# Transposing the two heads of an attention pair together, with each product in its own bank

## The chip, the cores and the metric

The kernel runs on one core of a Trainium2 chip. The metric is the device time of one execution in microseconds, compared as the median of the runs. Five engines appear below: PE (matrix products and transposes; PEld is its weight load), DVE (vector work), ACT (activations and copies), POOL (general work), and SP, which issues most transfers from HBM.

## The reference

One layer of a hybrid decoder on 256 tokens of width 1024, in fp32. Three mixers read one combined projection, a gated merge joins them, and two layer norms frame a large MLP.

```python
proj = x @ w_in[i]
aq, ak, av, iq, ik, iw, bq, bk, bv, cq, ck, cv = jnp.split(proj, SPLIT_POINTS, axis=-1)
o_a = dsa_mixer(...)        # 6 heads, 64 keys chosen by an indexer, one shared k and v
o_b = dilated_mixer(...)    # 4 slots, three dilated query groups over shared keys
o_c = moba_mixer(...)       # 6 heads, at 256 tokens plain causal attention
merged = (gates[:, :, 0] * (o_a @ w_br_a[i]) + gates[:, :, 1] * (o_b @ w_br_b[i])
          + gates[:, :, 2] * (o_c @ w_br_c[i]))
x = layer_norm(ALPHA * x + merged @ w_out[i], ln1_g[i], ln1_b[i])
h = jnp.square(jax.nn.relu(x @ w_up[i])) @ w_down[i]
ple = jax.nn.sigmoid(x @ w_ple_gate[i]) * (p[i] @ w_ple[i])
x = layer_norm(ALPHA * x + h + ple, ln2_g[i], ln2_b[i])
```

What the change touches is the end of each head's attention: the softmax's weights are transposed and multiplied with the values, 16 times (4 slots, 6 heads of `o_c`, 6 heads of `o_a`), two heads to a pair.

## The kernel before

Every fp32 matrix is split into a rounded high part and the rest (high on ACT, L75; low on DVE and POOL, L79), and a product is three matmuls in a reduced fp32 form. Weights arrive in units of 128 x 1024 through five `raw` buffers; a load waits until the split of the unit five places ahead of it has freed a buffer. `W.get` keeps the splits four units ahead of the product.

The program has stages. The first computes queries, keys and values from x, the indexer and its top 64 (a generator that DVE works off between other things), then the pairs: two of slots (`slots`, L351), three of `o_c` (L470), three of `o_a` (L487). Between the pairs stand gate products and branch products (`fill`, L234), so that PE has work while a pair's softmax runs on DVE and ACT. Then come the merge of the branches (`merge`, L561), the product with `w_out`, the first layer norm (`ln1`, L630) with its own transposes (L644), the gate of the per-layer embedding (`pg`), the MLP up (L693, L695) and down, and the second layer norm.

One head goes through these steps. `logits` (L264) fills two PSUM banks, one for each head of the pair. DVE adds the bias and takes the extreme; ACT takes the exponential; DVE the reciprocal; ACT scales the rows (L335). `attend` (L308) then transposes the three 128 x 128 blocks of the weights `P` into a bank (L314), ACT copies them to `pt` as the high part (L315), DVE makes the low part (L316), two matmuls form the product with the values (L318, L319), ACT copies the lower half of it out (L322), and DVE adds the halves (L323, L324) into the pair's `o`. When both heads are in `o`, `pair_out` (L326) splits `o` into `op`, which the branch products and the merge read.

PSUM has eight banks: three for `mm`, five named b0 to b4. Logits turn through b0, b1, b2; all transposes use b3; all products with the values use b4. So the second head's transposes wait until the first head's are out of b3.

The order on each engine is made by a scheduler that plays the program against its own idea of durations; `tc.keep_in_program_order` pins an instruction behind the one recorded before it on its engine, `tc.issue_after` behind a named one, and `high_priority` moves one ahead. All else is free to move, so that a change in one stage can move rows in the next.

Of the kernel before, what the change touches and what calls it, by code (L numbers as in the profile page):

```python
# [11 lines left out]
F32 = mybir.dt.float32  # L12
F32R = mybir.dt.float32r
ALU = mybir.AluOpType
# [6 lines left out]
S = 256  # L21
# [20 lines left out]
FIRST = 4  # L42
# [53 lines left out]
def hybrid_layer(ctx: ExitStack, tc: tile.TileContext, x0, xn, pT, wqk, wva, wvb, wg, wbc, wba,  # L96
                 wout, wup, wdq, wdn, wpg, wple, lnrow, rel, mask, out):
    nc = tc.nc
    pe, act, dve, pool = nc.tensor, nc.scalar, nc.vector, nc.gpsimd
# [10 lines left out]
    def turns(ids):  # L110

        while True:
            for i in ids:
                yield banks.tile([128, 512], F32, name=f"b{i}", tag=f"b{i}")

    ps_s, ps_t, ps_v, ps_a = turns((0, 1, 2)), turns((3,)), turns((4,)), turns((0, 1, 3, 2, 4))

    ident = keep.tile([128, 128], F32, name="ident")
    make_identity(nc, ident)
# [9 lines left out]
    t = banks.tile([128, 512], F32, name="b4", tag="b4")  # L129
# [43 lines left out]
    for t in TASKS:  # L173
# [4 lines left out]
        elif t in "gcao":  # L178
            u, w, n = {"g": (u_g, wg, 1024), "c": (u_bc, wbc, 640), "a": (u_ba, wba, 768),
                       "o": (u_out, wout, 1024)}[t]  # L180
# [14 lines left out]
    pts = [p1.tile([128, 2, 384], F32R, name=f"pt{i}") for i in range(2)]  # L195
# [84 lines left out]
    V = p1.tile([128, 2, 11, 128], F32R, name="V")  # L280
    iw = p1.tile([128, 2, 8], F32, name="iw")
    op = pm.tile([128, 8, 2, S], F32R, name="op")
# [22 lines left out]

    n_pt = [0]

    def attend(P, vh, o, h):  # L308

        pt = pts[n_pt[0] % 2]  # L310
        n_pt[0] += 1
        t = next(ps_t)
        for c in range(3):
            pe.transpose(t[:, 128 * c:128 * c + 128], P[:, 128 * c:128 * c + 128], ident)  # L314
        act.copy(pt[:, 0], t[:, 0:384])  # L315
        dve.tensor_tensor(pt[:, 1], t[:, 0:384], pt[:, 0].bitcast(F32), op=ALU.subtract)  # L316
        v = next(ps_v).rearrange("p (a s) -> p a s", a=2)
        pe.matmul(v, lhsT=V[:, 0, vh], rhs=pt[:, :, 0:256], start=True, stop=False)  # L318
        pe.matmul(v[:, :, 128:256], lhsT=V[:, 1, vh], rhs=pt[:, :, 256:384], start=False,  # L319
                  stop=True)  # L320
        x = wk2.tile([64, 2, S], F32, name="ov", tag="ov")
        act.copy(x, v[64:128])  # L322
        dve.tensor_tensor(x, v[0:64], x, op=ALU.add)  # L323
        dve.tensor_tensor(o[64 * h:64 * h + 64], x[:, 0], x[:, 1], op=ALU.add)  # L324

    def pair_out(o, kt):  # L326
        hi = act.copy(op[:, kt, 0], o)
# [3 lines left out]
    def scale_rows(P, den):  # L331
        r = sm.tile([128, 2], F32, name="r", tag="r")
        dve.reciprocal(r, den)
        for b in range(2):
            act.mul(P[:, QC[b]], P[:, QC[b]], r[:, b:b + 1])  # L335


    def head(s, t0, t1, vh, o, h):
        e = wk.tile([128, 384], F32, name="e", tag="e")
        mx = sm.tile([128, 2], F32, name="mx", tag="mx")  # L340
        den = sm.tile([128, 2], F32, name="den", tag="den")
        for b, t in enumerate((t0, t1)):
            dve.tensor_tensor_reduce(e[:, QC[b]], s[h][:, QC[b]], t, op0=ALU.add, op1=ALU.min,
                                     scale=1.0, scalar=-GONE, accum_out=mx[:, b:b + 1])
        for b in range(2):
            act.activation(e[:, QC[b]], e[:, QC[b]], AF.Exp, bias=mx[:, b:b + 1], scale=-1.0,
                           accum_out=den[:, b:b + 1])
        scale_rows(e, den)
        attend(e, vh, o, h)

    def slots(qs, k, Ts, vh, o):  # L351

        es = [wk2.tile([128, 3, 384], F32, name="eb", tag="eb") for _ in range(2)]
        mxs = [sm.tile([128, 2, 3], F32, name="mxb", tag="mxb") for _ in range(2)]
        for g in range(3):
            s = logits(qs[g], k)
            for h in range(2):
                for b, t in enumerate((Ts[h][:, g, 128:256], Ts[h][:, g, :])):
                    dve.tensor_tensor_reduce(es[h][:, g, QC[b]], s[h][:, QC[b]], t, op0=ALU.add,
                                             op1=ALU.min, scale=1.0, scalar=-GONE,  # L360
                                             accum_out=mxs[h][:, b, g:g + 1])
        for h in range(2):
            e = es[h]
            m = sm.tile([128, 2], F32, name="mx", tag="mx")
            den = sm.tile([128, 2], F32, name="den", tag="den")
            dve.tensor_reduce(m, mxs[h], axis=AX.X, op=ALU.min)
            for b in range(2):
                act.activation(e[:, :, QC[b]], e[:, :, QC[b]], AF.Exp, bias=m[:, b:b + 1],
                               scale=-1.0, accum_out=den[:, b:b + 1])
            pool.tensor_tensor(e[:, 0], e[:, 0], e[:, 1], op=ALU.add)  # L370
            added[0] = pool.tensor_tensor(e[:, 0], e[:, 0], e[:, 2], op=ALU.add).ins
            scale_rows(e[:, 0], den)
            attend(e[:, 0], vh + h, o, h)

# [9 lines left out]
    with ExitStack() as begin:  # L386
        st = begin.enter_context(tc.tile_pool(name="st", bufs=1, side="right"))
        sh, sl = (st.tile([128, KT, FIRST * 128], F32R, name=n) for n in ("sh", "sl"))
        g0 = G.rearrange("p i s -> p (i s)").rearrange("p (k c) -> p k c", k=KT)
        cut = [((0, 384), (384, 768)) if k == 0 else ((0, 768),) for k in range(KT)]  # L390
        with tc.high_priority(offset=1000):
            for k in range(KT):
                for i, (a, b) in enumerate(cut[k]):
                    e = nc.scalar if i else nc.sync
                    e.dma_start(g0[:, k, a:b], x0[k, :, a:b])
            for k in range(KT):
                act.copy(xh[:, k], g0[:, k, 0:S])
                for a, b in cut[k]:
                    a = max(a, S)
                    act.copy(sh[:, k, a - S:b - S], g0[:, k, a:b])  # L400
                dve.tensor_tensor(xl[:, k], g0[:, k, 0:S], xh[:, k].bitcast(F32), op=ALU.subtract)
                dve.tensor_tensor(sl[:, k], g0[:, k, S:], sh[:, k].bitcast(F32), op=ALU.subtract)
        first = [next(ps_s if f < 3 else ps_t)[:, 0:S] for f in range(FIRST)]
        for k in range(KT):
            for i, (w, x) in enumerate(((sh, xh), (sh, xl), (sl, xh))):
                for f in range(FIRST):
                    pe.matmul(first[f], lhsT=w[:, k, 128 * f:128 * f + 128], rhs=x[:, k],  # L407
                              start=k == i == 0, stop=k == KT - 1 and i == 2)
        iq = [q_pair(ps, 0.125) for ps in first]
    tp, wk, wk2, sm = (right(n, b) for n, b in (("tp", 3), ("wk", 3), ("wk2", 2), ("sm", 6)))  # L410
# [13 lines left out]
    for j in range(4):  # L424
        s = logits(iq[j], kI)
        r = wk2.tile([128, 768], F32, name="ri", tag="eb")
        r = r.rearrange("p (h k) -> p h k", h=2)
        for h in range(2):
            act.activation(r[:, h], s[h], AF.Relu)
            for b in range(2):  # L430
                n = 2 * j + h
# [15 lines left out]
    def opair():  # L447
        return wk2.tile([128, S], F32, name="o", tag="o")

    for j in range(2):  # L450
# [8 lines left out]
        o = opair()  # L459
# [10 lines left out]
    for j in range(3):  # L470
        ps = feat(13 + 2 * j)
        k = k_pair(ps)
        q = q_pair(feat(14 + 2 * j))
        s = logits(q, k)
        o = opair()
        for h in range(2):
            n = 2 * j + h
            if n % 3 == 0:
                T = toeplitz(18 + n, 1)
            head(s, T[:, n % 3, 128:256], T[:, n % 3], 5 + n, o, h)  # L480
            fill("g")
        pair_out(o, 5 + j)

# [2 lines left out]
    T = None  # L486
    for j in range(3):  # L487
        q = q_pair(feat(19 + j))
        s = logits(q, kA)
        o = opair()  # L490
        for h in range(2):
            n = 2 * j + h
            if n % 3 == 0:
                T = toeplitz(n, 1)
            ta = wk.tile([128, 384], F32, name="ta", tag="ta")
            with tc.issue_after(W.pool):
                pool.tensor_tensor(ta[:, 0:128], T[:, n % 3, 128:256], am[:, 0:128], op=ALU.add)
                pool.tensor_tensor(ta[:, 128:384], T[:, n % 3], am[:, 128:384], op=ALU.add)
            head(s, ta[:, 0:128], ta[:, 128:384], 0, o, h)
            fill("gg" if n == 0 else "gc")  # L500
        done = pair_out(o, j)
    fill("ggcc")
# [152 lines left out]
    for b in range(2):  # L655
        t = slice(b * 128, (b + 1) * 128)
# [31 lines left out]
    for f in range(32):  # L688
# [5 lines left out]
        for k in range(KT):  # L694
            pe.matmul(ps[:, :, 0], lhsT=lo[:, cs[k]], rhs=x1[:, :, k, 0], start=False,  # L695
                      stop=k == KT - 1)
# [3 lines left out]
        u, m = divmod(f, 4)  # L700
        if u >= QUADS:
            q = w2.tile([128, S], F32, name="q2", tag="q2")
            act.activation(q, r.rearrange("p b t -> p (b t)"), AF.Square)
            h = hT[:, f - 4 * QUADS]
# [21 lines left out]
        else:  # L726
            ts = [[qpool.tile([128, 2, S], F32R, name="q", tag="q")
                   .rearrange("p m (j t) -> p m j t", j=2) for _ in range(2)] for _ in range(2)]
# [61 lines left out]
    for x in order:  # L790
# [4 lines left out]
        else:  # L795
            i = x - NP + 2
# [20 lines left out]
    for i in range(early):  # L817
        x = order[i]
# [39 lines left out]
    for b, c, lo, hi in runs:  # L858
        cs = slice(*CUT[b][c])
        for i in range(lo, hi):  # L860
            h, l = ws[i]
# [102 lines left out]
```

## Time and profile before

| | |
|---|---|
| three runs | 434.8, 435.6, 436.42 us; median 435.6 |
| the profiled execution | 437.98 us |
| its span, first to last instruction | 436.2 us |
| granted TensorE clock over the span | 0.994 |
| busy PE, DVE, ACT, POOL | 425.1, 350.5, 276.2, 105.4 us |
| matmuls and transposes on PE | 2799 |

A row of a timeline has the start in us, the time, the engine, the line, the operation, what it writes and reads, and in square brackets the idle time ahead of it with what ended that. A matmul's own duration is longer than its step, since matmuls overlap; the step from start to start is what it costs PE.

### The profile page before, as it was taken

The page shows a single profiled execution, that of the slowest core. Times are in us where ns is not written, and L with a number is a line of the kernel's source. Part 1 is how long each engine was busy: PE and PEld are TensorE (multiplying, and loading weights), DVE is VectorE, ACT ScalarE, POOL GpSimd, SP SyncE. Part 2 cuts the span into 40 slices and gives each one's busy share as a digit, 9 for nine tenths or more (in the row PEclk, how much of TensorE's full clock was granted, in tenths as well). Part 3 has the DMA queues.
Part 4 walks back from the last instruction along what each step waited for, and adds up shares of the span by engine and source line. Part 5 has one row for each costly group of instructions (what it writes and reads, how often), then busy time and mean ns, then how long its engine had stood idle before and what let it go on. Part 6 is the DMA issues. An engine that isn't in the chain of part 4 may idle for free.

```text
span 436.2 us, 7669 instructions
## 1 busy us (share of the span) xinstructions
PE 425.1 (97%) x2799; PEld 386.0 (88%) x2799; DVE 350.5 (80%) x625; ACT 276.2 (63%) x490; POOL 105.4 (24%) x98
## 2 busy tenths in 40 slices
PE   8999999999999999999998999999999999999993
PEld 8999999999999999999886888888888888888882
DVE  5978987577476577879957779999988897998984
ACT  6775375586787777756524567788887855665500
POOL 2563355395434566400000000000100000000001
PEclk9999999999999999999999999999999999999997
DMA  8797756457654436455960875656795377758411
GB/s 298 291 326 234 230 173 191 150 189 250 183 151 145 128 109 187 144 192 178 400 246 0 288 237 185 187 180 203 277 268 187 115 207 269 200 192 278 155 41 57
DMA packets 27690, 86.39 MB, mean 198 GB/s; under 512 B 2884, under 2 KB 6892, under 8 KB 27268
## 3 DMA queue, kind: packets, MB, share of 16 engines
q1 hardware_dynamic: 25872, 79.54, 55.1%
q0 software_dynamic: 640, 2.17, 2.9%
q10 hardware_dynamic: 1140, 4.19, 2.6%
q8 instruction: 22, 0.36, 0.3%
q14 instruction: 16, 0.13, 0.1%
HBM read 83.99 MB, written 1.90 MB: 197 GB/s over the span
## 4 chain that ended last, share of the span: by engine, by line
PE 88%; DVE 5%; issue 3%; DMA 2%; POOL 0%; POOLq 0%; ACT 0%; DVEq 0%; ACTq 0%
PE mm L136 40%; PE b L136 18%; PE mm L693 13%; PE mm L695 7%; PE b L274 3%; PE b L407 3%; DMA raw<-in_wpg_dram 2%; PE b L314 1%; PE b L318 1%; DVE hT L79 1%; DVE st L611 1%; DVE Y L625 1%; PE b L131 1%; DVE G L570 1%; DVE Y L634 1%
## 5 line engine op out<-in xcount | busy, mean ns | idle before, releaser
L79 DVE TENSOR_TENSOR wlo<-raw,whi 128x1024 fp32r<-128x1024 f32 (+5 forms) x146 | 157.5, 1092 | 41.9 <-ACT whi L75 37.9
L75 ACT CAST whi<-raw 128x1024 fp32r<-128x1024 f32 (+3 forms) x146 | 146.1, 1011 | 48.8 <-PE b L136 11.7
L79 POOL TENSOR_TENSOR wlo<-raw,whi 128x384 fp32r<-128x384 f32 (+3 forms) x58 | 78.8, 1367 | 82.6 <-ACT whi L75 73.6
L136 PE MATMUL mm<-xl,whi 128*128 128x256 f32 x336 | 95.7, 285 | 0.0
L136 PE MATMUL mm<-xh,whi 128*128 128x256 f32 x336 | 95.3, 284 | 0.0
L136 PE MATMUL mm<-xh,wlo 128*128 128x256 f32 x336 | 95.0, 283 | 0.0
L136 PEld LDWEIGHTS mm<-xl,whi 128*128 128x128 f32 x336 | 63.3, 188 | 1.0
L693 PE MATMUL mm<-x,whi 128*128 128x512 f32 x256 | 64.1, 392 | 0.0
L136 PEld LDWEIGHTS mm<-xh,whi 128*128 128x128 f32 x336 | 63.3, 188 | 0.7
L136 PEld LDWEIGHTS mm<-xh,wlo 128*128 128x128 f32 x336 | 63.3, 188 | 0.3
L693 PEld LDWEIGHTS mm<-x,whi 128*128 128x128 f32 x256 | 46.1, 189 | 8.3
L136 PE MATMUL b<-whi,hT 128*128 128x512 f32 (+2 forms) x164 | 51.8, 381 | 0.0
L695 PEld LDWEIGHTS mm<-x,wlo 128*128 128x128 f32 x256 | 34.9, 190 | 2.5
L741 POOL DMA_DIRECT2D rows<-in_wdq_dram x4 | 3.6, 972 | 135.3 <-DVE wlo L79 81.9
L695 PE MATMUL mm<-x,wlo 128*128 128x256 f32 x256 | 35.7, 282 | 0.0
L136 PEld LDWEIGHTS b<-whi,hT 128*128 128x128 f32 x164 | 30.5, 188 | 5.8
L136 PE MATMUL b<-wlo,hT 128*128 128x512 f32 (+2 forms) x82 | 31.2, 381 | 0.0
L618 POOL TENSOR_TENSOR rs<-rs,half 128x1 f32<-128x1 f32 x4 | 4.1, 1031 | 103.3 <-DVE rs L617 103.3
L698 DVE TENSOR_REDUCE r<-mm 128x256 f32<-128x512 f32 x32 | 22.0, 688 | 4.9 <-PE mm L695 4.9
L136 PE MATMUL mm<-op,whi 128*128 128x256 f32 x128 | 23.6, 281 | 0.0
L136 PE MATMUL b<-whi,x 128*128 128x512 f32 x64 | 20.4, 394 | 0.0
L241 ACT ACTIVATE G<-mm 128x256 f32<-128x256 f32 x24 | 9.2, 381 | 17.4 <-PE mm L136 17.3
(162 smaller groups left out, 740.0 us busy)
## 6 DMA issues: line engine op xcount, KB each, us to landing
raw<-in_wup_dram SPq DMA_DIRECT2D x32, 512.0 KB
raw<-in_wg_dram SPq DMA_DIRECT2D x24, 512.0 KB
raw<-in_wqk_dram SPq DMA_DIRECT2D x18, 512.0 KB
raw<-in_wdn_dram SPq DMA_DIRECT2D x16, 512.0 KB
raw<-in_wdq_dram SPq DMA_DIRECT2D x12, 512.0 KB
raw<-in_wout_dram SPq DMA_DIRECT2D x8, 512.0 KB
raw<-in_wpg_dram SPq DMA_DIRECT2D x8, 512.0 KB
T<-tabd SPq DMA_DIRECT2D x24, 128.0 KB
```

The costliest lines, as they stand in the source:

```text
L75: nc.scalar.copy(hi, r)
L79: low = e.tensor_tensor(lo[:, c], r[:, c], hi[:, c].bitcast(F32), op=ALU.subtract)
L131: pe.transpose(t[:, 0:128], ident, ident)
L136: m = pe.matmul(ps, lhsT=a[x], rhs=b[y], start=first and i == 0, stop=last and i == 2)
L241: act.activation(G[:, n_g[0]], ps, AF.Tanh, scale=0.5)
L274: m = pe.matmul(ss[h][:, QC[b]], lhsT=q[d, x, c], rhs=k[d, y, 0:128 * (b + 1)], start=i == 0, stop=i == 2)
L314: pe.transpose(t[:, 128 * c:128 * c + 128], P[:, 128 * c:128 * c + 128], ident)
L318: pe.matmul(v, lhsT=V[:, 0, vh], rhs=pt[:, :, 0:256], start=True, stop=False)
L407: pe.matmul(first[f], lhsT=w[:, k, 128 * f:128 * f + 128], rhs=x[:, k], start=k == i == 0, stop=k == KT - 1 and i == 2)
L693: pe.matmul(ps, lhsT=hi[:, cs[k]], rhs=x1[:, :, k], start=k == 0, stop=False)
L695: pe.matmul(ps[:, :, 0], lhsT=lo[:, cs[k]], rhs=x1[:, :, k, 0], start=False, stop=k == KT - 1)
L698: dve.tensor_reduce(r, ps.rearrange("p b a t -> p b t a"), axis=AX.X, op=ALU.add)
```

## The change

`attend` takes both heads. It first transposes all blocks of both (the later head first, and of each head the blocks 1, 2, 0), every transpose but the very first pinned behind the one before it. Then each head is copied, split and multiplied as before, but the product with the values takes the bank that held that head's transposes: transposes and products turn through b3 and b2, and the logits use b0, b1, b4. `head` no longer calls `attend`; the loops call it once for a pair, after the second head's softmax. The slots' two heads do the same.

```diff
-    ps_s, ps_t, ps_v, ps_a = turns((0, 1, 2)), turns((3,)), turns((4,)), turns((0, 1, 3, 2, 4))
+    ps_s, ps_t, ps_a = turns((0, 1, 4)), turns((3, 2)), turns((0, 1, 3, 2, 4))
...
-    def attend(P, vh, o, h):
+    def attend(heads, o):
 
-        pt = pts[n_pt[0] % 2]
-        n_pt[0] += 1
-        t = next(ps_t)
-        for c in range(3):
-            pe.transpose(t[:, 128 * c:128 * c + 128], P[:, 128 * c:128 * c + 128], ident)
-        act.copy(pt[:, 0], t[:, 0:384])
-        dve.tensor_tensor(pt[:, 1], t[:, 0:384], pt[:, 0].bitcast(F32), op=ALU.subtract)
-        v = next(ps_v).rearrange("p (a s) -> p a s", a=2)
...
+        ts = []
+        for i, (P, vh, h) in enumerate(heads):
+            t = next(ps_t)
+            for c in (1, 2, 0):
+                m = pe.transpose(t[:, 128 * c:128 * c + 128], P[:, 128 * c:128 * c + 128], ident)
+                if i or c != 1:
+                    tc.keep_in_program_order(m)
+            ts.append(t)
+        for t, (P, vh, h) in zip(ts, heads):
+            pt = pts[n_pt[0] % 2]
+            n_pt[0] += 1
+            act.copy(pt[:, 0], t[:, 0:384])
+            dve.tensor_tensor(pt[:, 1], t[:, 0:384], pt[:, 0].bitcast(F32), op=ALU.subtract)
+            v = next(ps_t).rearrange("p (a s) -> p a s", a=2)
...
-        attend(e, vh, o, h)
+        return e
...
-            attend(e[:, 0], vh + h, o, h)
+        attend([(es[h][:, 0], vh + h, h) for h in (1, 0)], o)
...
-            head(s, T[:, n % 3, 128:256], T[:, n % 3], 5 + n, o, h)
+            e = head(s, T[:, n % 3, 128:256], T[:, n % 3], h)
+            heads = [(e, 5 + n, h)] + (heads if h else [])
+            if h:
+                attend(heads, o)
             fill("g")
```

No instruction is added or removed on PE, DVE, ACT or POOL; the scheduler's order is what differs. Three places matter below. In these rows the line numbers of the change are those of its own file (L324 and L325 are the former L318 and L319, L329 and L330 the former L323 and L324, L334 the former L328, L646 the former L634, L623 the former L611, L656 the former L644), and a number behind `b_` tells bank tiles apart.

The first is PE at the last pair, where the second head's transposes and both products stand among the branch products. Before, the first head's product and behind it the second head's transposes:

```order
L136 MATMUL mm<-xh,whi 128x256
L318 MATMUL b_2634<-pt_116,V 128x512
L319 MATMUL b_2634<-pt_116,V 128x2x128
L314 MATMUL b_2713<-ident,e 128x128 x3
L136 MATMUL mm<-xh,wlo 128x256
```

Now, the same place in the change, the six transposes in one run:

```order
L136 MATMUL mm<-xl,whi 128x256
L136 MATMUL mm<-xh,whi 128x256
L314 MATMUL b_2700<-ident,e 128x128 x3
L314 MATMUL b_2704<-ident,e 128x128 x3
L136 MATMUL mm<-xh,wlo 128x256
```

The products follow there some 25 rows later, three matmuls apart from each other, where before the first stood ahead of the second head's transposes:

```order
L324 MATMUL b_2710<-pt_116,V 128x512
L325 MATMUL b_2710<-pt_116,V 128x2x128
L136 MATMUL mm<-op,wlo 128x256
L136 MATMUL mm<-op,whi 128x256 x2
L324 MATMUL b_2719<-pt_117,V 128x512
L325 MATMUL b_2719<-pt_117,V 128x2x128
```

The second place is DVE behind these products. Before:

```order
L323 TENSOR_TENSOR ov<-b_2719,ov 64x512
L254 SCALAR_TENSOR_TENSOR G<-G,mm 128x512
L324 TENSOR_TENSOR o<-ov 64x256
L255 TENSOR_TENSOR G<-G 128x256
L254 SCALAR_TENSOR_TENSOR G<-G,mm 128x512
L328 TENSOR_TENSOR op<-o,op 128x256
```

Now:

```order
L329 TENSOR_TENSOR ov<-b_2710,ov 64x512
L329 TENSOR_TENSOR ov<-b_2719,ov 64x512
L254 SCALAR_TENSOR_TENSOR G<-G,mm 128x512
L330 TENSOR_TENSOR o<-ov 64x256 x2
L254 SCALAR_TENSOR_TENSOR G<-G,mm 128x512
L255 TENSOR_TENSOR G<-G 128x256
L334 TENSOR_TENSOR op<-o,op 128x256
```

One head's two additions, which were done some rows earlier, now stand ahead of the last `o`.

The third place lies after the stage that the diff touches: the first layer norm. DVE before (`Y` is the layer norm's input, `b_2936` to `b_2939` the four sums of the product with `w_out`, the `wlo` rows splits of weights):

```order
L79 TENSOR_TENSOR wlo<-raw,whi 128x1024 x4
L634 SCALAR_TENSOR_TENSOR Y<-PL,b_2936 128x512
L634 SCALAR_TENSOR_TENSOR Y<-PL,b_2937 128x512
L611 BN_STATS st<-Y 128x6 x2
L634 SCALAR_TENSOR_TENSOR Y<-PL,b_2938 128x512
L616 BN_AGGR mv<-st 128x2
```

and now:

```order
L79 TENSOR_TENSOR wlo<-raw,whi 128x1024 x3
L646 SCALAR_TENSOR_TENSOR Y<-PL,b_2936 128x512
L646 SCALAR_TENSOR_TENSOR Y<-PL,b_2937 128x512
L623 BN_STATS st<-Y 128x6
L79 TENSOR_TENSOR wlo<-raw,whi 128x1024
L623 BN_STATS st<-Y 128x6
L646 SCALAR_TENSOR_TENSOR Y<-PL,b_2938 128x512
```

The fourth split has moved behind two sums and one set of statistics. On PE in the same place, before (`mm<-..,ph` is the product of the embedding, `x_3147` the normed and transposed x):

```order
L644 MATMUL b_3211<-ident,Y 128x128 x4
L136 MATMUL mm<-whi,ph 128x512
L136 MATMUL mm<-wlo,ph 128x512
L136 MATMUL mm<-whi,pl 128x512
L136 MATMUL mm<-whi,ph 128x512
L136 MATMUL mm<-wlo,ph 128x512
L136 MATMUL mm<-whi,pl 128x512
L644 MATMUL b_3220<-ident,Y 128x128 x4
L136 MATMUL b_3311<-whi,x_3147 128x512
L136 MATMUL b_3311<-wlo,x_3147 128x512
L644 MATMUL b_3263<-ident,Y 128x128 x4
```

and now:

```order
L136 MATMUL mm<-whi,pl 128x512
L656 MATMUL b_3211<-ident,Y 128x128 x4
L656 MATMUL b_3220<-ident,Y 128x128 x4
L136 MATMUL b_3311<-whi,x_3147 128x512
L136 MATMUL b_3311<-wlo,x_3147 128x512
L656 MATMUL b_3263<-ident,Y 128x128 x4
```

The six embedding matmuls that stood between the first two groups of transposes now stand ahead of both. Behind this point the order on PE, DVE, ACT, POOL and SP is the same as before.

More of the change, by code (lines that the diff above doesn't have):

```diff
@@ L306, in hybrid_layer @@
     n_pt = [0]
-    def attend(P, vh, o, h):
-        pt = pts[n_pt[0] % 2]
-        n_pt[0] += 1
-        t = next(ps_t)
-        for c in range(3):
-            pe.transpose(t[:, 128 * c:128 * c + 128], P[:, 128 * c:128 * c + 128], ident)
-        act.copy(pt[:, 0], t[:, 0:384])
-        dve.tensor_tensor(pt[:, 1], t[:, 0:384], pt[:, 0].bitcast(F32), op=ALU.subtract)
-        v = next(ps_v).rearrange("p (a s) -> p a s", a=2)
[L318 to L324, printed above, removed]
+    def attend(heads, o):
[13 more added lines that the diff above has]
+            v = next(ps_t).rearrange("p (a s) -> p a s", a=2)
+            pe.matmul(v, lhsT=V[:, 0, vh], rhs=pt[:, :, 0:256], start=True, stop=False)
+            pe.matmul(v[:, :, 128:256], lhsT=V[:, 1, vh], rhs=pt[:, :, 256:384], start=False,
+                      stop=True)
+            x = wk2.tile([64, 2, S], F32, name="ov", tag="ov")
+            act.copy(x, v[64:128])
+            dve.tensor_tensor(x, v[0:64], x, op=ALU.add)
+            dve.tensor_tensor(o[64 * h:64 * h + 64], x[:, 0], x[:, 1], op=ALU.add)
     def pair_out(o, kt):
@@ L335, in scale_rows, with head @@
             act.mul(P[:, QC[b]], P[:, QC[b]], r[:, b:b + 1])
-    def head(s, t0, t1, vh, o, h):
+    def head(s, t0, t1, h):
         e = wk.tile([128, 384], F32, name="e", tag="e")
@@ L402, in hybrid_layer @@
                 dve.tensor_tensor(sl[:, k], g0[:, k, S:], sh[:, k].bitcast(F32), op=ALU.subtract)
-        first = [next(ps_s if f < 3 else ps_t)[:, 0:S] for f in range(FIRST)]
+        first = [next(p)[:, 0:S] for p in (ps_s, ps_s, ps_s, ps_t)]
         for k in range(KT):
@@ L498, in hybrid_layer @@
                 pool.tensor_tensor(ta[:, 128:384], T[:, n % 3], am[:, 128:384], op=ALU.add)
-            head(s, ta[:, 0:128], ta[:, 128:384], 0, o, h)
+            e = head(s, ta[:, 0:128], ta[:, 128:384], h)
+            heads = [(e, 0, h)] + (heads if h else [])
+            if h:
+                attend(heads, o)
             fill("gg" if n == 0 else "gc")
```

## The prediction

> **What bounds the kernel now.** I read the page's shares and its chain first, then PE's waits, then five windows cut where the stages change, then the timelines inside the windows in which PE is idle.
>
> ```profile
> PE 425.1 (97%) x2799; PEld 386.0 (88%) x2799; DVE 350.5 (80%) x625; ACT 276.2 (63%) x490; POOL 105.4 (24%) x98
> PE 88%; DVE 5%; issue 3%; DMA 2%; POOL 0%; POOLq 0%; ACT 0%; DVEq 0%; ACTq 0%
> PE b L644 <- DVE Y L625: 1.8, 2, 1.3
> 17.00:198.00 181.00, 181.00 (x1529) 175.67 (x1528) 134.56 (x345) 121.83 (x259) 92.03 (x76) 1.00 0.59 187
> 198.00:228.00 30.00, 30.00 (x155) 25.70 (x155) 24.99 (x37) 14.53 (x21) 0.37 (x1) 1.00 0.79 298
> 228.00:238.00 10.00, 8.23 (x43) 6.16 (x42) 8.20 (x15) 3.75 (x8) 1.64 (x2) 1.00 0.00 0
> 238.00:419.00 181.00, 181.00 (x918) 154.50 (x917) 161.47 (x192) 123.35 (x182) 3.57 (x4) 1.00 0.65 207
> ```
>
> PE carries 88% of the chain, and its one wait behind the start is for the first layer norm, 1.8 us in two pieces. The windows (length, then the busy time of PE, PEld, DVE, ACT and POOL, clock, DMA share, GB/s) say the same by stage: all 181 us of attention and all 181 us of the MLP have PE busy at full clock. Only the ten us around the layer norm hold 10.00 - 8.23 = **1.77 us of idle PE**. So a change in the attention stage can gain in three ways only: less PE work, less of these 1.77 us, or (as a loss) new idle time.
>
> **Part one, the transposes themselves.** The edit moves 48 transposes from 8 groups of one, 8 of two and 8 of three into runs of six. What a run costs PE is read from starts.
>
> ```profile
> 93.53 0.28 PE L136 MATMUL mm<-xh,whi 128*128 128x256 f32 x1
> 93.65 0.28 PE L136 MATMUL mm<-xh,wlo 128*128 128x256 f32 x1
> 93.77 0.27 PE L314 MATMUL b<-ident,eb 128*128 128x128 f32 x1
> 93.80 0.37 PE L136 MATMUL mm<-xl,whi 128*128 128x256 f32 x1
> 94.00 0.38 PE L314 MATMUL b<-ident,eb 128*128 128x128 f32 x2
> 94.14 0.36 PE L136 MATMUL mm<-xh,whi 128*128 128x256 f32 x1
> 94.34 0.28 PE L136 MATMUL mm<-xh,wlo 128*128 128x256 f32 x1
> ...
> 119.05 0.49 PE L314 MATMUL b<-ident,e 128*128 128x128 f32 x3
> 119.29 0.37 PE L136 MATMUL mm<-xh,whi 128*128 128x256 f32 x1
> 119.50 0.28 PE L136 MATMUL mm<-xh,wlo 128*128 128x256 f32 x1
> ```
>
> A plain matmul of 256 columns steps by 0.12 (93.53 to 93.65). From 93.65 to 94.00 there are two of them and one transpose: 0.35 - 0.24 = 0.11. From 94.00 to 94.34, one matmul and two transposes: 0.34 - 0.12 = 0.22. From 119.05 to 119.50, one and three: 0.45 - 0.12 = 0.33. So a transpose costs 0.11 alone, in a pair or in three; entering a run is free to the rounding of these rows, at most 0.01 us. The change saves about 15 entries (24 runs become 9, because one group still breaks into three and three): **0 to -0.15 us, taken as -0.1**. The Trainium skill, in "TensorE: Matmul & The Clock Gate", section "Back-to-back issue gap", puts a sustained matmul of 128 columns at about 81 ns. By it a longer run would save 27 ns at each of 15 more inner steps, an estimate of 0.4 us; the 109 ns between transposes inside the runs here (0.38 less one duration of 0.27) speaks against it.
>
> **Part two, the wait that the change adds.** Now the first of six waits for the later head, and PE's whole queue (gate and branch products) stands behind it. Before, the slack between the scaling of a head's rows and its first transpose was:
>
> ```profile
> 166.17 0.81 ACT L335 ACTIVATE e<-e,r 128x128 f32<-128x128 f32 x2 [0.77 <-DVE r L333]
> 167.38 0.27 PE L314 MATMUL b<-ident,e 128*128 128x128 f32 x1
> ...
> 178.13 0.80 ACT L335 ACTIVATE e<-e,r 128x128 f32<-128x128 f32 x2
> 180.84 0.27 PE L314 MATMUL b<-ident,e 128*128 128x128 f32 x1
> ```
>
> 0.40 us in the tightest pair I found (167.38 - 166.98) and 1.9 us in the last, which is typical (180.84 - 178.93). The new run stands near the second head's old place, not the first's (in the last pair at the rows of the order where its three stood), so the first head has more to spare than before, and the second head about what the first had. The products follow some 4 us of matmuls behind the run. I cost this at **nothing**, from 0 in the typical pair to perhaps 0.5 us a pair where other work on ACT and POOL is late; the cover is that slack.
>
> **Part three, behind the last pair.** The merge reads `op` of that pair.
>
> ```profile
> 191.40 0.40 PE L318 MATMUL b<-pt,V 128*128 128x512 f32 x1
> 193.07 0.68 DVE L323 TENSOR_TENSOR ov<-b,ov 64x512 f32<-64x512 f32 x1
> ...
> 194.38 0.42 DVE L324 TENSOR_TENSOR o<-ov 64x256 f32<-64x256 f32 x1
> 194.83 0.41 ACT L327 CAST op<-o 128x256 fp32r<-128x256 f32 x1 [2.30 <-DVE o L324]
> 196.07 0.63 PE L136 MATMUL mm<-op,whi 128*128 128x256 f32 x4
> ```
>
> Before, `op` was ready at 195.24 and PE first read it at 196.07. Now two more additions stand ahead of the last `o`: an L323 (0.61, from 193.07 to the next start on DVE) and an L324 (some 0.3 of its 0.42). Nothing lets DVE begin earlier: the split and the gate's step ahead of them are the same rows. So `o` ends 0.9 later, at 195.7, and `op` is ready at 196.1. On PE the last product stands 0.4 us of matmuls further ahead of that reading; counted from the start of the merge PE is there at about 195.8. **A wait of 0.3 us**, between 0 and 0.6. The weight splits behind it on DVE are delayed by these 0.9 us and by the wait, an estimate of 1 to 2 us. The window from 198 to 228 shows that none of them kept PE waiting before (30.00 of 30.00), but not how near they came: between nothing and 2 us. I take nothing, since the nearest row, `op`, had 0.8 us to spare (196.07 - 195.24) and the planner keeps the splits four units ahead of the product. They also move the loads that wait for their buffers, which is taken up below.
>
> **Part four, the layer norm, where the idle time is.** The chain there:
>
> ```profile
> 212.47 8.91 DMA raw<-in_wpg_dram
> 221.48 1.06 ACT whi L75
> 222.56 0.06 DVE wlo L79
> ...
> 223.70 1.28 DVE Y L634 x2
> 224.98 1.20 DVE st L611 x2
> 226.18 0.59 DVE Y L634
> ...
> 233.07 0.75 DVE Y L625
> ...
> 219.00 6.06 PE L136 MATMUL b<-hT,q 128*128 128x512 f32 x26
> 222.56 1.23 DVE L79 TENSOR_TENSOR wlo<-raw,whi 128x1024 fp32r<-128x1024 f32 x1 [4.90 <-ACT whi L75]
> 233.87 0.66 PE L644 MATMUL b<-ident,Y 128*128 128x128 f32 x4 [1.32 <-DVE Y L625]
> ```
>
> DVE stood 4.90 us in front of one weight's split, which waited for a transfer, while the sums that the layer norm needs were done: in the 26 matmuls from 219.00 (0.227 apart) the first bank is complete at about 220.5, the second at 221.2, the third at 222.8. In the change two sums (0.60 each) and one set of statistics (0.60) run in that gap, from 220.5 to 222.5, ahead of the split. Then, if the transfer lands as before, split to 223.7, the other statistics to 224.3, and the third sum starts at 224.3 instead of 226.18: 1.9 us earlier. With it moves all that follows on DVE, so that the `Y` of 233.07 to 233.82 is ready at about 232.0.
>
> PE's own road to that place starts at the embedding products:
>
> ```profile
> 229.59 0.66 PE L644 MATMUL b<-ident,Y 128*128 128x128 f32 x4 [0.45 <-DVE Y L625]
> 230.34 0.59 ACT L646 CAST x<-b 128x512 fp32r<-128x512 f32 x1 [0.57 <-PE b L644]
> ```
>
> PE had drained at 229.14 (229.59 less the 0.45 idle), so the next matmul could have started at 229.0: in the row of 26 the step is 0.227 and the last one's own time 0.39, which is 6.06 less 25 steps. The other six embedding products now come before both groups of transposes: 229.0 + 6 x 0.227 + 0.2 (parts one and three) = 230.55. The two groups take 4 x 0.11 each, to 231.4. ACT's copy of the first, which PE needs next, starts 0.75 after its group (230.34 - 229.59) and takes 0.59: 231.9. Two matmuls later PE is at the third group at 232.35, where DVE has finished `Y`. That is 233.87 - 232.35 = **1.5 us earlier**, parts one and three included. What is late next is PE itself. Behind this place the order is the old one and PE was full, so the gain stays, and the last stage moves as a whole.
>
> **The sum and its ends.** -1.5 us. It cannot be better than the whole idle time and part one, -1.77 - 0.15 = -1.9 (and 0.16 for each of the two drains in front of that idle time, -2.2). The other end hangs on the transfer of 212.47. By part three it is issued 1.5 to 2 us later, as its buffer comes free later, and the queue was full:
>
> ```profile
> 218.00:220.00 2.00, 2.00 (x11) 1.65 (x10) 0.00 (x0) 0.00 (x0) 0.00 (x0) 1.00 1.00 404
> ```
>
> A unit of 128 x 1024 in fp32 is 512 KB, 1.3 us at 404 GB/s, so most of the 8.91 us were spent behind other bytes. Over 198 to 228 the share of DMA was 0.79, so 6 us of transfer time were free, and a later issue need not land later. At worst it lands 2 us later: the third sum is then at 226.3, as before, and the sum of the change is +0.2 us (part three less part one). I take the landing as it was.
>
> On the profiled execution, 437.98 us, of which 436.2 are the span, this gives 436.5. The three runs have a median of 435.6, 2.4 below that execution; the same subtraction gives **434.1 us**.
>
> **The rivals.**
>
> *The transfer lands later.* For it: the loads wait for splits that DVE now does later, and the share of DMA was 1.00 from 218 to 220, just ahead of the landing. Against it: the free 6 us. Anything between half of the gain and none: 434.8 to 435.8, say 435.6. Chance 0.23.
>
> *PE waits for the later head.* The mechanism is part two: an in-order queue held by the first of six. Its place are the eight groups, its price what the later head's scaling is behind PE. It decides from 0.5 us at every group: 8 x 0.5 = 4 us, less the 1.5, is 2.5 slower, 438.1. For it: the pair with 0.40 us, where the second head's exponentials and scaling ran late. Against it: the 1.9 us, and no wait of PE in all 181 us. Chance of this size or more 0.12; of a smaller one that eats the gain, up to 437, another 0.07.
>
> *The transposes lower the clock.* A rule that speaks against runs of transposes would show as a lower granted clock. The kernel's start has such a run:
>
> ```profile
> L131 PE MATMUL b<-ident 128*128 128x128 f32 x13 | 3.0, 425 | 1.7 <-POOL ident masks.py:199 1.7
> ```
>
> There a transpose takes 425 ns, in the attention stage 270 to 280 (the rows of 167.38 and 93.77), at a clock of 1.00 in the window. Thirteen slow ones stand at the start of an idle engine. If each run of six set PE back to that rate for as long as it holds them (3.0 us, half of it lost), eight runs would cost 12 us: 446. The present runs of three show none of it, so chance 0.01. The Trainium skill, "TensorE: Matmul & The Clock Gate", section "Part 4: PE-mode transpose", says that a transpose "doesn't count as PE-busy the same way" for that clock; the trace's windows, at 1.00 with 48 transposes in them, agree only in that such short runs do not matter.
>
> *The change does not do what it says.* One group of eight breaks into three and three around a few matmuls; by part one that costs 0.01 us, and no chance is set aside for it.
>
> **How the numbers follow.** Forecast, 0.57: 433.0 to 435.2, about 434.1. The later transfer, 0.23. Waits, 0.19. Clock, 0.01. The range from 432.7 to 437.1 leaves out the large waits and the clock (0.13) and what a new set of runs may differ from these three (theirs spread over 1.6 us). 0.5% of 435.6 is 2.2 us, about what a measurement of this kernel can tell from no change: faster means under 433.4, slower over 437.8. The sum's own bound, -1.9 to -2.2, only just reaches the first, so faster is only the lower part of the forecast's spread, 0.22; slower is the large waits and the clock, 0.13; the rest, 0.65, is within.
>
> **What would show it right or wrong.** PE's waits: the entry at the layer norm falls from 1.8 to under 0.6 us, and the window around it has PE nearly full. DVE: the first two sums start ahead of the late split, and the third near 224.3. Part two fails if L314's successor shows idle time for ACT's scaling; part three if the merge does not wait for `op`, or waits over 0.6. The prediction as a whole is wrong if the attention window grows by over 0.5 us, or if the transfer's row lands as much later as its issue moved.

## The result and the profile after

The change makes the kernel slower: a median of 438.97 us over ten runs (436.83 to 440.99) against 435.43 over ten runs of before, a ratio of 1.0085 with a 95% interval of 1.0064 to 1.0106. The forecast was 434.1, the range 432.7 to 437.1. The ten times lie in two groups, five from 436.83 to 438.26 and five from 439.68 to 440.99. Two executions of a kernel below (`b_own_rows`) took 703.85 and 2392.72 us and are left out of its ratio.

Four views of the changed kernel's profile follow: the page's busy times, its chain by engine, PE's waits behind the start, and the same windows as before (length, busy PE, PEld, DVE, ACT, POOL, clock, DMA share, GB/s).

```profile
PE 424.3 (98%) x2799; PEld 385.1 (89%) x2799; DVE 355.3 (82%) x625; ACT 274.7 (63%) x490; POOL 107.5 (25%) x98
PE 92%; DMA 2%; issue 2%; DVE 2%; ACT 1%; POOLq 0%; POOL 0%; SPq 0%; DVEq 0%
PE b L274 <- DVE q L218: 1.1, 1, 1.1
PE b L136 <- ACT x L658: 0.3, 1, 0.3
17.00:198.00 181.00, 179.92 (x1519) 174.46 (x1518) 138.05 (x344) 120.37 (x259) 94.41 (x77) 1.00 0.59 187
198.00:228.00 30.00, 30.00 (x158) 25.81 (x157) 27.48 (x40) 14.41 (x21) 1.01 (x1) 1.00 0.80 298
228.00:238.00 10.00, 9.71 (x50) 7.73 (x49) 7.84 (x15) 4.99 (x9) 1.00 (x1) 1.00 0.00 0
```

Two things are to be seen. At the layer norm (the last window) PE is idle for 10.00 - 9.71 = 0.29 us where it was 1.77, about the 1.5 us that were forecast. But the attention stage, full before, now has a wait: 1.1 us in front of one head's logits (L274), for its queries (L218). And this profiled execution took 436.83 us, the shortest of the ten, while the profiled execution of before took 437.98, more than any of its timed runs. Comparing these two traces alone would call the change a gain. So both kernels were profiled again, several times.

The chain of the changed kernel between 94 and 108 us (start, us, what) says where the 1.1 us come from:

```profile
94.74 0.66 PE b L314 x6
95.39 1.14 PE mm L136 x10
96.54 5.08 DMA pr<-in_pT_dram
...
101.64 0.63 ACT ph L472
...
102.30 0.69 DVE pl L473
102.99 1.20 DVE ov L329 x2
104.19 0.34 DVE k L229
...
104.55 0.43 DVE o L330
...
105.00 1.12 DVE o L330
106.13 0.74 DVE wlo L79
106.86 0.08 DVE op L334
...
107.13 0.42 DVE q L218
...
107.59 0.96 PE b L274 x12
```

`pr` is the load of the embedding's input; it borrows a buffer of the slots (tag `eb`), so it can be issued only when the transposes of the last pair of slots have read that buffer: now the run of six. ACT casts it (`ph`), and in ACT's queue this cast stands ahead of the copies of that pair's products; DVE's split of it stands ahead of the pair's additions. Behind these come the next pair's keys (L229) and queries (L218), which PE needs at 106.5. This place, the last pair of slots, is a fourth one beside the three that were named ahead of the prediction. Here it is in another execution of before (`b_again`): the two heads' transposes, the load, its cast, and then DVE's timeline:

```profile
93.82 0.38 PE L314 MATMUL b<-ident,eb 128*128 128x128 f32 x2
95.35 0.38 SPq L465 DMA_DIRECT2D pr<-in_pT_dram  x1
99.49 0.49 PE L314 MATMUL b<-ident,eb 128*128 128x128 f32 x3
101.27 0.62 ACT L466 CAST ph<-pr 128x512 fp32r<-128x512 f32 x1 [3.21 <-DMA pr<-in_pT_dram]
101.92 0.69 DVE L467 TENSOR_TENSOR pl<-pr,ph 128x512 fp32r<-128x512 f32 x1 [2.04 <-ACT ph L466]
102.53 0.68 DVE L323 TENSOR_TENSOR ov<-b,ov 64x512 f32<-64x512 f32 x1
103.14 0.54 DVE L316 TENSOR_TENSOR pt<-b,pt 128x384 fp32r<-128x384 f32 x1
103.60 0.41 DVE L229 TENSOR_TENSOR k<-mm,k 128x256 fp32r<-128x256 f32 x1
103.93 0.41 DVE L324 TENSOR_TENSOR o<-ov 64x256 f32<-64x256 f32 x1
104.26 0.82 DVE L79 TENSOR_TENSOR wlo<-raw,whi 128x640 fp32r<-128x640 f32 x1
105.00 0.41 DVE L218 SCALAR_TENSOR_TENSOR q<-mm,q 128x256 fp32r<-128x256 f32 x1
```

Before, the first head's transposes were done at 94.20 and the load went out at 95.35; the second head's followed at 99.49. Now the run of six lies between these places, and the load goes out at 96.54; its cast starts 0.37 us later than in `b_again`. DVE waited for the same cast before. But from the start of `pl` to the end of `q` it took 105.41 - 101.92 = 3.49 us, and now 107.55 - 102.30 = 5.25: the second head's `ov` and `o` and the pair's `op` have come ahead of `q`, and one `o` took 1.12 us. PE started the logits at 106.42 there, 1.0 after `q` (in the first trace of before it was 1.7). The change has used up this spare time on both sides: a little by a later load (0.4 us) and more by the work ahead of `q` (1.8 us).

### The profile page after: what moved, and what is told of

The parts are those of the page before. It is cut to its first block, busy times and chain, and to the rows that moved or that the text cites. A ratio compares the mean times of both kernels' runs of the same rounds, so it can differ in the third digit from the quotient of the medians.

```text
span 435.0 us, 7673 instructions
## 1 busy us (share of the span) xinstructions
PE 424.3 (98%) x2799; PEld 385.1 (89%) x2799; DVE 355.3 (82%) x625; ACT 274.7 (63%) x490; POOL 107.5 (25%) x98
## 4 chain that ended last, share of the span: by engine, by line
PE 92%; DMA 2%; issue 2%; DVE 2%; ACT 1%; POOLq 0%; POOL 0%; SPq 0%; DVEq 0%
PE mm L136 40%; PE b L136 23%; PE mm L705 14%; PE mm L707 7%; PE b L274 3%; PE b L413 2%; DMA G<-in_x_dram 1%; PE b L314 1%; DMA pr<-in_pT_dram 1%; PE b L324 1%; PE b L325 0%; DVE o L330 0%; DVE ov L329 0%; POOLq L972 0%; POOL rs L630 0%
## 5 line engine op out<-in xcount | busy, mean ns | idle before, releaser
L79 POOL TENSOR_TENSOR wlo<-raw,whi 128x384 fp32r<-128x384 f32 (+3 forms) x58 | 79.0, 1369 | 81.4 <-ACT whi L75 72.3
```

The lines of the kernel that those rows point to most:

```text
L79: low = e.tensor_tensor(lo[:, c], r[:, c], hi[:, c].bitcast(F32), op=ALU.subtract)
```

## The experiments

Kernels whose names begin with `a` are made from the changed kernel, with `b` from before. Ratios are those of the comparison with runs of before on the same chip; where only one execution was profiled, there is a time and no ratio.

**The two kernels unaltered, and a buffer of its own for `pr`.** `a_own` and `b_own` differ from after and before in one line:

```diff
-    pr = wk2.tile([128, 2, S], F32, name="pr", tag="eb")
+    pr = p1.tile([128, 2, S], F32, name="pr")
```

The load then goes out at 10 us and `ph` is cast at 18 to 19 us.

> The changed kernel unaltered, to see how its executions differ: the ten times spread over 4.2 us (436.83 to 440.99), those of before over 1.6. Theory (a late load): in the profile of the fastest, PE stood 1.1 us at 106.5 for a head's queries, behind ACT's cast of the embedding input (ph), which waited 3.7 us for the load of pr. If that wait sets the spread, an execution of about 438 to 441 shows the same place with a longer wait of PE, 2 to 4 us, and the load landing later by as much. Rival (elsewhere): the wait at 106 stays at 1.1 us and the rest of the time is lost at the merge, the layer norm or by a lower clock.

> The kernel before unaltered, to see where its executions of 435.4 are shorter than the profiled one of 437.98. If the layer norm's transfer lands earlier there, the 1.8 us wait of PE at its transposes is shorter, and what the change can gain at that place is less than the 1.5 us I counted; if the profiled execution was only slower all over, the wait is 1.8 us again.

> The changed kernel with a buffer of its own for the load of pr, so that it no longer waits for the transposes of the last pair of slots; ph is then cast at about 20 us. Theory (a late load): the cast's wait of ACT at 98 to 101.6 goes, PE's wait at 106.5 goes with it, and the time falls by 3 to 5 us, to 434 to 436. Rival (DVE's order: both halves' additions now stand ahead of the next pair's keys and queries): the wait stays near 1 us and the time falls by under 1.5 us, to 437.5 or above. Rival (elsewhere): 438.5 to 439.5.

> The kernel before with the same buffer for pr, the control of a_own. Before, PE did not wait at that place, so by the theory this is worth nothing there: within 0.3% of before, 434.5 to 436.5. If it falls by as much as a_own does, the load was a cost of both kernels and doesn't explain the difference.

`a_again` took 437.89 us, with a wait of 0.4 at the queries and 1.1 at the layer norm: another mixture than in the first trace, and no answer on the upper group. `b_again` took 435.71, and its window at the layer norm is

```profile
228.00:238.00 10.00, 10.00 (x52) 7.94 (x51) 7.82 (x14) 5.69 (x10) 0.99 (x1) 1.00 0.00 0
```

**no idle time at all**. The 1.77 us on which the forecast rested were in the first trace of before and are not in this one, nor in those of `b_own` and `b_own_rows` below.

`a_own` gave 436.54, ratio 1.0022 (1.0001 to 1.0042): some three quarters of the loss are gone, and its trace has no wait in the attention stage. `b_own` gave 435.21, ratio 0.9989 (0.9974 to 1.0003): the load cost nothing before. So the place at 106 is the larger part of the loss: 2.4 us between the medians, short of the 3 to 5 us that the theory expected to come back.

**One place undone at a time.** In `a_slot` only the last pair of slots goes one head at a time again, in the new banks; `pr` keeps its old buffer. In `a_last` only the last pair of all does.

```diff
 a_slot
-        attend([(es[h][:, 0], vh + h, h) for h in (1, 0)], o)
+            if alone:
+                attend([(e[:, 0], vh + h, h)], o)
+        if not alone:
+            attend([(es[h][:, 0], vh + h, h) for h in (1, 0)], o)
...
-        slots(qs, k, Ts, 1 + 2 * j, o)
+        slots(qs, k, Ts, 1 + 2 * j, o, j == 1)
 a_last
-            heads = [(e, 0, h)] + (heads if h else [])
-            if h:
+            heads = [(e, 0, h)] + (heads if h and j < 2 else [])
+            if h or j == 2:
                 attend(heads, o)
```

> The changed kernel once more. Its times lie in two groups, five near 438.2 and five near 440.5, with granted clocks of 0.995 and 0.991; both traces so far are of the first group. If this is one of the second: theory, a longer wait at the head's queries (106) by 2 us and, behind it, a stretch with a granted clock under 1. Rival: the clock falls at another wait, or with none.

> The changed kernel with the two heads of the last pair of slots transposed and multiplied one by one again, in the new banks; all other pairs stay grouped. The load of pr keeps its old buffer, which comes free 1 us earlier, and on DVE the next pair's keys and queries come ahead of the second head's additions again. Theory (that one place costs 2 to 3 us): 436 to 437, no wait of PE at 106, and no time near 440. Rival (the load's buffer alone matters, not the order): a wait of 0.5 us or more stays, 437.5 or above.

> The changed kernel with the two heads of the last pair of all (ahead of the merge) transposed and multiplied one by one again. Theory (the additions of two heads ahead of the last o delay the merge's splits, so the loads of w_out and of the embedding's gate come 1 to 2 us later, and PE waits 0.8 us at the layer norm): the load of w_out is issued at about 203.5 instead of 205.4, the waits at the layer norm fall under 0.4, and the time falls by 0.5 to 1.2 us, to 437.8 to 438.5. Rival (the six embedding products ahead of both groups of transposes are the cause): the waits stay at 0.8, the time at 439.

> Both: a buffer of its own for pr, and the last pair one by one. If the two places are all that the change lost, this is the 435.2 of the kernel before with the same buffer, 434.8 to 435.7; if a loss remains elsewhere in the attention stage, 436 or above.

`a_slot`: 1.0016 (1.0006 to 1.0027), no wait at 106 and no time above 438.06. Grouping this one pair costs the larger part. ACT still waited 2.4 us for the load, but as long as in the two traces of before (2.5 and 3.2), and `pl` started at 101.86, as in `b_again`: undoing the pair brings back the time of the load and the order ahead of `q` together, so this run does not tell the two apart. That the order weighs more is argued from the 0.4 and 1.8 us above, and is not tested alone. `a_last`: 1.0047 (1.0030 to 1.0064), with a wait of 1.0 at 106 and 1.7 at the layer norm, so its mechanism failed: the load of `w_out` went out at 206.32, not at 203.5 (PE was 1.4 us later than in the first trace after already at 82 us, which does not make up for it). Its ratio lies below the changed kernel's all the same; none of its six executions has a granted clock under 0.995, of which more below. `a_own_last`, 1.0023 (1.0004 to 1.0041), is `a_own` again. The additions of the last pair are not what is left. `a_again2` was of the lower group, 437.75, with 1.2 at 106.

**The layer norm.** What waiting of PE is left in `a_own` behind the start lies there. In `a_own` PE waits 0.5 us for `Y` and 0.3 for the first copy of x. In ACT's timeline (ACTq is its queue of transfers) and SP's, the second unit of the gate's weights (`wpg`):

```profile
213.26 0.33 ACTq L610 DMA_DIRECT2D rows<-in_lnrow_dram  x1
213.46 0.33 SPq L71 DMA_DIRECT2D raw<-in_wpg_dram  x1
222.06 1.05 ACT L75 CAST whi<-raw 128x1024 fp32r<-128x1024 f32 x1 [4.79 <-DMA raw<-in_wpg_dram]
```

The unit needs 8.6 us from issue to cast, right behind a load of 1 MB (`rows`, the norm's scale and shift) from ACT's queue. In `b_own` it was the other way round, the unit at 211.70 and the rows at 212.23, and ACT cast it at 216.02, without having waited over 0.2. In `b_again` the two went out 0.1 us apart, the rows first, and it took 7.0; in the first trace of before they were as close, and it took 9.0 (212.47 to 221.48). So the kernel before meets the slow case too, in some executions. Two kernels tell the order of the six embedding products from this transfer. `a_own_ple` pins the products between the groups of transposes, as before. `a_own_rows` holds the load of the rows behind the cast of the gate's first unit, and the scheduler then restores the old order by itself; `b_own_rows` is its control.

```diff
 a_own_rows, b_own_rows
-        nc.scalar.copy(hi, r)
+        self.casts[i] = nc.scalar.copy(hi, r).ins
...
-        row_load(rows1, 0)
...
     def ln1(b, c, acc):
+        if b == c == 0:
+            with tc.issue_after(W.casts[u_pg[0]]):
+                row_load(rows1, 0)
 a_own_ple
+                with ExitStack() as held:
+                    if b == c == 1:
+                        held.enter_context(tc.issue_after(turned[3]))
+                    prod(ps, (ph[:, k, t], pl[:, k, t]), (wp[k][0][:, cs], wp[k][1][:, cs]),
+                         k == 0, k == 1)
```

(`turned[3]` is the last transpose of the first group.)

> The changed kernel once more, for a trace of the second group of its times (near 440.5, clock 0.991). Theory: a stretch of PE with a granted clock under 1 behind one of its waits, worth some 2 us beside the waits themselves. If it is of the first group again (near 438), nothing is told of that.

> The changed kernel with a buffer of its own for pr and, at the layer norm, the last six embedding products pinned between the first two groups of transposes, as before the change. Theory (the transfer of the gate's second unit lands 2 to 3 us later): PE still waits 0.5 to 1 us there, for Y or for the first copy of x, and the time stays at that of a_own, 0.2% above before. Rival (the order of these six products costs the time): no wait is left and the time falls by 0.6 to 0.8 us, to before or under it.

> The changed kernel with a buffer of its own for pr, and the 1 MB load of the layer norm's rows held behind the cast of the gate's first unit; the scheduler then puts the gate's second split and the six embedding products where they stood before the change. Theory (the late transfer): the unit lands some 4 to 5 us after its issue instead of 8.5, the waits at the layer norm go, and the time falls by 0.7 to 1.3 us under a_own, to the level of b_own. Rival (it is late because of its issue alone): it lands as late, the waits stay or grow to 1.5 us.

> The kernel before with both: the control. Where its transfer landed early in most executions, this is worth 0 to 0.4 us under b_own, 434.6 to 435.3, with a smaller spread; if it equals a_own_rows within 0.15%, the change's own content (transposes in runs of six, products in the transposes' banks) is worth nothing that can be measured.

`a_own_ple`: 1.0016 (1.0005 to 1.0027), not told apart from `a_own` by the time. In its trace the wait for the copy of x is gone and that for `Y` is 0.2; the transfer still took 8.8 us. `a_own_rows`: **1.0003 (0.9995 to 1.0011)**, and no wait of PE behind the start. Its rows of the two queues and the cast:

```profile
213.26 0.33 SPq L72 DMA_DIRECT2D raw<-in_wpg_dram  x1
215.40 0.34 ACTq L611 DMA_DIRECT2D rows<-in_lnrow_dram  x1
217.78 1.05 ACT L76 CAST whi<-raw 128x1024 fp32r<-128x1024 f32 x1 [1.34 <-DMA raw<-in_wpg_dram]
```

The unit is issued as late as in `a_own` and is cast 4.5 us later instead of 8.6. (The intervals of `a_own_ple` and `a_own_rows` just overlap; it is the traces that tell them apart.) `b_own_rows` gave 0.9994 (0.9985 to 1.0003), with a median of 435.08 us on the chip on which `a_own_rows` had 435.10. With both places mended, the changed kernel and before are the same within what these runs resolve, and neither beats before by an amount that can be told from nothing.

`a_again3`: 438.19, with 0.7 us at 106 and 1.4 at the layer norm. Such waits do not make up the whole of a single time: PE reaches the logits near 82 us between 81.2 and 82.0 in the four traces of kernels from before, and between 81.4 and 82.8 in the fourteen from the changed one.

**The square, and the upper group.** `a_rows` has the rows held back and `pr` in its old buffer.

> The changed kernel with only the load of the rows held back; pr keeps its old buffer. With a_own (only pr) and a_own_rows (both) this completes the square. Theory (two separate losses that add): the waits at the layer norm go, PE's wait of 0.4 to 1.2 us at the head's queries stays, and the time is 0.2 to 0.5% above before, 436.2 to 437.5. Rival (one loss, the delay at 106 also makes the loads late): the layer norm's waits stay.

> The changed kernel, timed on the same chip as a_rows, with more executions. The traces account for some 2 us above before (437.8 to 438.2); the five times near 440.5 of the first ten are not explained. If they belong to the kernel, about half of these executions are over 439.5 with a clock of 0.991; if they were of that chip or hour, none or few are, and the difference from before is 0.4 to 0.7%.

> For a trace of an execution near 440.5. Theory: a granted clock under 1 for some 3 us behind a wait of PE. Rival: no dip, but a wait that the traces so far do not have.

> For a trace of an execution near 440.5, as with the run before. Theory: a granted clock under 1 for some 3 us behind a wait of PE. Rival: no dip, but a wait that the traces so far do not have.

| | `pr` in its old buffer | `pr` in its own |
|---|---|---|
| rows early | 1.0085 (1.0064 to 1.0106) | 1.0022 (1.0001 to 1.0042) |
| rows held back | 1.0039 (1.0023 to 1.0055) | 1.0003 (0.9995 to 1.0011) |

The trace of `a_rows` has 1.1 us at 106 and none at the layer norm: two losses in separate places. Their sizes do not simply add (0.63% for `pr` with the rows early, 0.36% with them held back), and how often the clock falls, below, may be why; no run shows it. `a_again5` and `a_again6` took 437.61 and 437.57, with 0.6 and 1.4 us at 106. `a_again4` gave 1.0103 (1.0086 to 1.0119); of its six times four lie above 440, one at 439.1, and its trace is of one of 440.29. PE's wait, windows of 2 us, and PE's timeline there:

```profile
PE b L274 <- DVE q L218: 1.9, 1, 1.9
106.00:108.00 2.00, 0.87 (x8) 0.67 (x6) 1.97 (x4) 0.67 (x3) 1.02 (x1) 1.00 0.04 8
108.00:110.00 2.00, 1.24 (x13) 1.02 (x13) 1.53 (x4) 2.00 (x4) 0.97 (x1) 0.79 0.38 82
110.00:112.00 2.00, 2.00 (x11) 2.00 (x10) 1.80 (x6) 0.57 (x3) 2.00 (x2) 0.50 0.57 199
112.00:114.00 2.00, 2.00 (x17) 2.00 (x16) 0.80 (x6) 2.00 (x10) 0.22 (x1) 0.85 0.72 260
108.76 1.31 PE L274 MATMUL b<-k,q 64*128 64x128 f32 x12 [1.89 <-DVE q L218]
...
110.38 0.41 PE L136 MATMUL mm<-xh,wlo 128*128 128x256 f32 x1
110.59 0.41 PE L136 MATMUL mm<-xl,whi 128*128 128x256 f32 x1
```

The wait is 1.89 us, and behind it the granted clock falls to 0.50: a matmul of 256 columns steps by 0.21 instead of 0.12. From 106 to 114 the clock's loss is 2 x (0.21 + 0.50 + 0.15) = 1.7 us, on top of the wait. The load `pr` took 5.90 us in this execution where it took 5.08 in the first, so a transfer 0.8 us longer went with 0.8 + 1.7 us (in `b_again` it took as long, and PE did not wait). In the other traces waits of up to 1.4 us left the clock at 1.00. The wait, the clock's loss and 0.9 us at the layer norm make 4.5 of the 4.9 us by which this execution lies above the median of before.

This is one trace of the upper group. Its other times fit as far as the clock is on record: four of the five in the first ten have 0.991, but the fifth, 439.68, has 0.994, and `a_last` took 439.58 at 0.995 by longer waits alone. The place at 106 does not explain every low clock either. `a_own` has one time of 440.51 at 0.992 and `a_own_last` two, 440.13 and 438.55, at 0.990, though their traces have no wait there; `a_rows`, which keeps that wait, has only one low clock in eight (439.0 at 0.989). What sets how often the clock falls stays open, and with it how much of the square's ratios is clock and how much is waiting.

## Why the prediction was wrong

**Part two is the step that failed.** "I cost this at **nothing** [...] the cover is that slack" looked at PE's wait for the later head, and no trace shows that one: PE's waits name no L314. What was not costed is what stands behind the grouping on the other engines. The first head's transposes moved later, and with them the release of its buffer, which a load was waiting for; that load's cast stands in ACT's queue ahead of the pair's copies; and the second head's additions moved ahead of the next pair's queries on DVE. All of that was in the order of the instructions; I read the order at the last pair and at the layer norm only, and took the slack of two places for that of eight. "The new run stands near the second head's old place" is right for the last pair (186.81 against 187.08 us) and wrong for the last pair of slots, where the run starts at 94.58 and the two heads' transposes before at 93.77 and 99.67: the first head's are delayed and the second head's come 5 us early. The place with a transfer in its chain had 1.0 and 1.7 us to spare in the two traces of before; in the seven traces of the change PE waits there for 0.4 to 1.9 us, and in the one with 1.9 another 1.7 us went to the lowered clock.

**Part four had the right mechanism on the wrong base.** In the first trace after, the wait fell as forecast (9.71 against 8.23): two sums stand ahead of the late split, and the third starts at 224.96, where 224.3 was given. But the sum was made against one execution that was 2.4 us longer than the median of the runs, and those 2.4 us were subtracted as if they lay everywhere. Most lay where the gain was to come from: `b_again`, 435.71 us, has 10.00 of 10.00 busy there. A typical execution of before had nothing to give back. Of the 4.87 us between 434.1 and 438.97, by an estimate from the medians, 1.33 are this gain that was not there (435.43 less 434.1), 2.43 the place at 106 (438.97 less 436.54 of `a_own`), and 1.11 the rest (436.54 less 435.43), which holding the rows back removes.

**"I take the landing as it was" failed too**, in the direction of the rival that got 0.23. By the traces of `b_again` and `a_own`, the unit is issued at 212.29 and 213.46 and cast at 219.25 and 222.06: 1.2 us later out, 2.8 later there. Against the profiled execution that the forecast was made on it is 1.8 later out in the first trace after (214.26 against 212.47) and only 0.6 later there (222.12 against 221.48), near the forecast; that execution was slow at this place already. I had looked for a later issue, not for what the unit meets when it is late: the 1 MB of rows ahead of it. Holding the rows back took the loss away. Why the issue is late can be read from DVE. The unit goes out 0.02 us behind the third of four splits of `w_out` (`hT`); in `b_again` two steps of the merge (`q`, L575) stand between the second and the third, in `a_own` four (`q`, L587), and that is 0.67 of the 1.2 us. Undoing the last pair (`a_own_last`) left the four where they were. Why the scheduler puts four there is not shown.

**Part one** cannot be told from nothing, and its range began there. Between the logits near 82 us and the 26th matmul from the end of the product with `w_out` (219.00 in the trace before), in before and then in `a_own`, neither with a wait of PE in between:

```profile
81.97 0.95 PE L274 MATMUL b<-k,q 64*128 64x128 f32 x12
...
81.73 0.95 PE L274 MATMUL b<-k,q 64*128 64x128 f32 x12
...
218.74 6.05 PE L136 MATMUL b<-hT,q 128*128 128x512 f32 x26
```

it is 219.00 - 81.97 = 137.03 us and 218.74 - 81.73 = 137.01. That is 0.02, where 0 to 0.15 was given, and no more than the scatter: up to the end of that product the four traces of before, `b_again`, `b_own` and `b_own_rows` have 143.04 to 143.09 us, those of `a_own`, `a_own_ple` and `a_own_rows` 143.07 to 143.09.

**Part three** was close: the merge's wait of 0.3 is not there. ACT's cast of `op` ends at 196.44 in the trace after, and PE's four matmuls that read it start at 196.49: the 0.83 us to spare are used up, and PE does not wait.

**The clock rival** had 0.01, for the transposes as a cause; the granted clock did fall, by way of a wait of PE. The Trainium skill, "TensorE: Matmul & The Clock Gate", section "HAM oscillation — how this bites in real kernels", puts the limit at idle gaps over some 3.4 us; here one gap of 1.89 us was enough, and gaps of up to 1.4 were not. The measurement decides, though it is a single trace.

## What to carry to other kernels

Where work of several items is grouped, ask at every place what the first item's last read released, and who waits in order behind the one that waits for it; a typical slack is no cover for the place with a transfer in its chain. Before a wait is booked as a gain, compare the profiled execution with the runs: what it is longer by may be that very wait. Here it took repeated traces of the unaltered kernels before the edits could be read.

## What the runs showed of the hardware

A wait of PE of 1.89 us was followed by some 3.4 us with a granted clock of 0.50 (1.7 us lost at half speed, `a_again4`, one trace), while one of 1.4 us was not (`a_again6`). The same transfer of 512 KB took at most 4.3 us from issue to cast when issued 0.5 us ahead of a 1 MB load from another engine's queue (`b_own`), and 8.6 when issued 0.2 behind it (`a_own`); issued 0.1 behind it, it took 7.0 (`b_again`) and 9.0 (before). An addition of 64 x 256 on DVE took 1.12 us instead of 0.42 in the trace after, while POOL ran a split from 104.79 to 105.86; it ended 0.26 behind that split. In `a_again4` the same addition took 1.12 us beside a split of POOL from 105.96 to 107.02, and ended at 107.30. The Trainium skill, "SBUF — State Buffer", section "SBUF: two separate sides", says that the two engines' shared port is locked for a whole instruction, not divided; these rows agree with it.
